# Gate and up of 17 feed-forward tiles as seven half-size block products, with two of the weight sums made by adding DMAs

## The chip, the cores and the metric

The kernel runs on one core of a Trainium2 chip. The metric is the device time of one execution in microseconds (us). Names of engines: PE is TensorE (matrix products; PEld is its loading of the stationary operand), DVE is VectorE, ACT is ScalarE, POOL is GpSimd, SP is SyncE, which here only issues transfers (DMAs).

## What is computed

One layer of a hybrid decoder for 512 tokens of width 1024, in float32. Two feed-forward blocks with 2816 hidden units stand around a mixing block of sixteen heads. The change is in the gate and up products of the two feed-forward blocks (`x @ wg` and `x @ wu`).

```python
def swiglu(x, wg, wu, wd):
    return (jax.nn.silu(x @ wg) * (x @ wu)) @ wd
...
        h = h + 0.5 * swiglu(rmsnorm(h, ffn1_norm[i]), ffn1_wg[i], ffn1_wu[i], ffn1_wd[i])
        a = rmsnorm(h, mix_norm[i])
        u = a @ w_in[i]
...
        h = h + mixed @ w_out[i]
        h = h + 0.5 * swiglu(rmsnorm(h, ffn2_norm[i]), ffn2_wg[i], ffn2_wu[i], ffn2_wd[i])
        gate = jax.nn.sigmoid(rmsnorm(h, ple_gate_norm[i]) @ ple_w_gate[i])
        e = rmsnorm(p[i] @ ple_w_proj[i], ple_norm[i])
        h = h + gate * e
```

## The kernel before

Every float32 product is made of three passes in the type float32r: an operand is split into a high part `hi` (a cast, on ScalarE) and a low part `lo` (operand minus `hi`, on VectorE), and `passes` gives high times high, high times low and low times high, which add up in one PSUM bank.

In `ffn` the 2816 hidden units are 22 tiles of 128, in chunks of 8, 7 and 7. For a tile and for each of gate and up, `weights` loads the [1024, 128] block of the weights in one 512 KB DMA on SP into a staging buffer (tag `st`, 3 slots), and `split` makes `hi` and `lo` (4 slots each). 24 matmuls (8 blocks of 128 inputs times 3 passes), each over all 512 tokens, fill one PSUM bank of the tag `gub` (4 banks). `hidden` then makes silu(gate) * up and splits it. After a chunk, the down projection runs over the chunk's tiles into the four banks of the tag `acc`, and the result is added to `h`. In the first block the first two tiles are computed while x arrives, and x is not yet normalized: the factor 1/rms of the tokens is multiplied onto the gate product (`R`, a row), and the other factor of it comes in after the down projection.

```python
        hi, lo = (self.nc.tile(self.sb, (P, 1024), F32R, tag, 4)[:, :a * n].rearrange("p (a c) -> p a c", a=a)
                  for tag in ("hi", "lo"))
```

The program isn't issued as it is written. `Plan.record` keeps every instruction with a cost and latencies from a table, and `Plan.issue` makes one list schedule of it: each engine takes, of the instructions whose operands and buffer slots are there in this model, the one that stands first in the program. The order of each engine's instructions is fixed by this; on the chip they run in that order, each when its operands are there. For this reason all instructions stand under one line of the profile, L296, and have to be told apart by the tiles that they write and read: `gub<-x,hi` is a gate or up product, `acc<-hi,k` or `acc<-hi,pt` one of the down projection, `lo<-st,hi` a split on VectorE, `hi<-st` a split on ScalarE. The profile leaves out buffer numbers, and a digit at the end of a tag with them (`x` is `x8`, `w` is `w2`, `k` is `k4`).

GpSimd does small arithmetic on statistics (`s`) and issues a handful of small DMAs at the start.

## Time and profile before

| what | value |
| --- | --- |
| time, three runs | 1122.46, 1122.73 and 1217.59 us; median 1122.73 us |
| span of the profiled execution | 1122.3 us |
| outside the span, against the median | 0.4 us |
| TensorE busy | 1106.8 us, 99%, 5635 matmuls |
| VectorE busy | 587.6 us, 52% |
| ScalarE busy | 493.9 us, 44% |
| GpSimd busy | 161.7 us, 14% |

The profiled execution is listed by its span alone, which is 0.2 and 0.4 us below the two lower runs; sums are made against the span, and the 0.4 us to the median are added. A busy engine isn't one at its peak: the records of matmuls overlap (a matmul of 512 columns has a record of 0.39 us), and what counts is the distance from one to the next. The granted clock is the share of TensorE's full speed of 2.4 GHz that it was given.

### The profile page before, as it was taken

The numbers are of one execution on the slowest core, as the hardware profiler recorded it, in microseconds if no ns is written. First come the engines' busy times: TensorE is split into PE (matmuls) and PEld (weight loads), VectorE is DVE, ScalarE is ACT, GpSimd is POOL, SyncE is SP. The second block draws the span as 40 slices with busy tenths as digits, with TensorE's granted clock in tenths as the row PEclk, the third lists the DMA queues.
The fourth block names the chain that finished last, engine by engine and source line by source line (L and its number), as shares of the span: only waits on it lengthen the run. The fifth ranks groups of instructions, "written<-read, shape, count | busy, mean of one in ns | idle before, by whom it ended". The sixth has DMA issues, their size and how long they took to land.

```text
span 1122.3 us, 15134 instructions
## 1 busy us (share of the span) xinstructions
PE 1106.8 (99%) x5635; PEld 941.9 (84%) x5635; DVE 587.6 (52%) x1121; ACT 493.9 (44%) x1017; POOL 161.7 (14%) x312
## 2 busy tenths in 40 slices
PE   9999999999999999999999999999999999999998
PEld 6888888888888988898999888888888888888887
DVE  5443343334443687889889887733333323333353
ACT  5332132222321767978988964522222221222252
POOL 2000000000000167553344511200000000000010
PEclk9999999999999999999999999999999999999999
DMA  7432333333343631312102232433223323332221
GB/s 215 123 97 94 94 94 95 100 88 112 95 107 84 213 119 39 76 30 58 36 25 72 100 125 73 137 103 102 94 75 113 94 85 103 104 103 85 90 80 66
DMA packets 143657, 106.60 MB, mean 95 GB/s; under 512 B 12624, under 2 KB 125296, under 8 KB 143584
## 3 DMA queue, kind: packets, MB, share of 16 engines
q1 hardware_dynamic: 143392, 105.55, 31.3%
q8 instruction: 45, 0.74, 0.3%
q14 instruction: 28, 0.23, 0.1%
q0 software_dynamic: 192, 0.08, 0.1%
HBM read 101.29 MB, written 4.33 MB: 94 GB/s over the span
## 4 chain that ended last, share of the span: by engine, by line
PE 87%; DVE 4%; POOL 2%; ACT 2%; issue 2%; DMA 1%; SPq 0%; POOLq 0%; ACTq 0%
PE gub L296 49%; PE acc L296 39%; DVE k L296 1%; POOL s L296 1%; ACT w L296 1%; DVE w L296 1%; POOL r L296 1%; POOL w L296 1%; ACT k L296 1%; DVE s L296 1%; DVE lo L296 0%; DMA st<-in_w_in 0%; DVE x L296 0%; DMA spill<-k 0%; DMA ident<-in_ident 0%
## 5 line engine op out<-in xcount | busy, mean ns | idle before, releaser
L296 PE MATMUL gub<-x,hi 128*128 128x512 f32 x1376 | 424.7, 390 | 0.0
L296 ACT CAST hi<-st 128x1024 fp32r<-128x1024 f32 (+4 forms) x171 | 166.1, 981 | 502.4 <-PE acc L296 181.6
L296 PEld LDWEIGHTS gub<-x,hi 128*128 128x128 f32 x1376 | 258.3, 188 | 53.1
L296 DVE TENSOR_TENSOR lo<-st,hi 128x1024 fp32r<-128x1024 f32 (+4 forms) x171 | 192.6, 1134 | 194.4 <-ACT hi L296 189.7
L296 PE MATMUL gub<-x,lo 128*128 128x512 f32 x688 | 267.8, 389 | 0.0
L296 PE MATMUL acc<-hi,x 128*128 128x256 f32 (+3 forms) x720 | 181.9, 329 | 0.0
L296 PE MATMUL acc<-hi,k 128*128 128x512 f32 (+1 forms) x512 | 166.0, 391 | 2.2 <-DVE k L296 2.0
L296 PEld LDWEIGHTS gub<-x,lo 128*128 128x128 f32 x688 | 129.2, 188 | 26.9
L296 POOL TENSOR_SCALAR s<-s 128x1 f32<-128x1 f32 (+3 forms) x65 | 18.6, 286 | 801.6 <-ACT k L296 755.9
L296 PEld LDWEIGHTS acc<-hi,x 128*128 128x128 f32 x720 | 123.3, 190 | 5.2
L296 PE MATMUL acc<-hi,pt 128*128 128x512 f32 x384 | 122.4, 395 | 0.0
L296 PE MATMUL acc<-lo,x 128*128 128x256 f32 (+3 forms) x360 | 117.5, 328 | 0.0
L296 PEld LDWEIGHTS acc<-hi,k 128*128 128x128 f32 x512 | 96.7, 190 | 19.8 <-issue 2.2
L296 PE MATMUL acc<-lo,k 128*128 128x512 f32 (+1 forms) x272 | 103.2, 383 | 0.0
L296 DVE TENSOR_TENSOR w<-w,gub 128x512 f32<-128x512 f32 x42 | 28.9, 688 | 135.6 <-PE gub L296 135.6
L296 PEld LDWEIGHTS acc<-hi,pt 128*128 128x128 f32 x384 | 72.3, 188 | 16.9
L296 PE MATMUL acc<-lo,pt 128*128 128x512 f32 x192 | 75.7, 394 | 0.0
L296 PEld LDWEIGHTS acc<-lo,x 128*128 128x128 f32 x360 | 68.2, 190 | 2.7
L296 ACT ACTIVATE w<-w,s 128x128 f32<-128x128 f32 (+1 forms) x96 | 53.8, 563 | 9.7 <-DVE s L296 9.3
L296 PEld LDWEIGHTS acc<-lo,k 128*128 128x128 f32 (+1 forms) x272 | 50.0, 184 | 8.5
L296 PE MATMUL gub<-ident,w 128*128 128x128 f32 (+2 forms) x316 | 52.4, 274 | 0.6 <-ACT w L296 0.2
L296 POOL TENSOR_TENSOR s<-s,mhalf 128x1 f32<-128x1 f32 (+3 forms) x61 | 49.4, 810 | 4.1
(154 smaller groups left out, 1198.9 us busy)
## 6 DMA issues: line engine op xcount, KB each, us to landing
st<-in_ffn_wg SPq DMA_DIRECT2D x42, 512.0 KB, 3.8
st<-in_ffn_wu SPq DMA_DIRECT2D x42, 512.0 KB, 3.9
st<-in_ffn_wd SPq DMA_DIRECT2D x40, 512.0 KB, 3.6
st<-in_w_in SPq DMA_DIRECT2D x48, 128.0 KB, 2.5
st<-in_w_in SPq DMA_DIRECT2D x8, 512.0 KB, 3.8
st<-in_w_out SPq DMA_DIRECT2D x8, 512.0 KB, 3.8
st<-in_ple_w_gate SPq DMA_DIRECT2D x8, 512.0 KB, 3.9
k<-in_x SPq DMA_DIRECT2D x16, 128.0 KB, 4.1
```

The costliest lines, as they stand in the source:

```text
L296: getattr(getattr(self.nc, op.eng), m)(*a, **k)
```

## The change

The 22 tiles become 11 pairs of 256 hidden units, p = 0 to 10, in chunks of pairs 0 to 3, 4 to 7 and 8 to 10. Pairs 0 to 2 of the first block and 0 and 1 of the second are computed as before (`gate_up`: 4 products of 24 matmuls over 512 tokens; the text calls them classic pairs). The other 17 pairs (8 and 9 of them) go through `gate_up7`.

There, the weights of a pair (gate and up side by side) and the transposed input are each cut into 2 by 2 blocks: the 1024 inputs into two halves, the 256 hidden units into two halves of 128, the 512 tokens into two halves of 256. Seven products of sums of blocks take the place of eight products of blocks. A product is 24 matmuls (gate and up, 4 blocks of 128 inputs, 3 passes) over 256 tokens, into one bank; a pair has 168 of them. The results are put together from the seven products by additions and subtractions on VectorE. The seven operands of the input (`x_operands`) are made once for each block, from a copy of the input that is put together by copying DMAs on SP (high part) and adding DMAs on GpSimd (low part).

For a pair, five 512 KB blocks of the weights are loaded on SP (`s`, `s3`, `a11`, `a22`, `a12`; the first two load the same block, quarter (1, 0)). Two DMAs issued by GpSimd read a block from DRAM and add it to what lies in the buffer (`accum_op`): quarter (0, 0) to `s3`, quarter (1, 1) to `s`. VectorE adds `a11` and later `a12` to `s`. Seven operands are split (`w7`, `w5`, `w6`, `w1`, `w4`, `w2`, `w3`, in the order in which their products run), each with one cast and one subtraction of 128x1024.

The tag `st` has 7 slots and holds the low parts too (before: 3 and 4); `k4` has 17 in place of 14. The down projection does the same products, two hidden tiles at a time, with a factor of 0.5; the row 1/rms is now multiplied onto gate and up both, in classic pairs, and onto the input's blocks for the others. To free buffers, the normalized embedding `e` is written to DRAM after its product and read back in the last stage, where its factor and gain are now multiplied on. The weights of gate and up come in a new layout from DRAM (`_quarters`), so that each block is one DMA of 4 KB rows. In the planner's table a matmul's cost changes, a GpSimd DMA costs 900 and the result of an adding DMA is due 4500 later. `L296` becomes `L304`.

```diff
-ST = 3
+ST = 7
 REST = 4
 STOP = "stop"
 PACE = 5250.0
 POOL_LO = ()
-K4 = 14
+K4 = 17
+CLASSIC = 2
...
-            return f * max(m / 1.2, self.cols(outs[0]) / 2.4) + 2.5
+            return f * max(m / 1.2 + 2.5, self.cols(outs[0]) / 2.4 + 13.5)
...
+        if method == "dma_start":
+            return 900.0
...
+        if "accum_op" in k:
+            op.lat = dict.fromkeys(op.lat, 4500.0)
...
+        hi, lo = (x[:, :a * n].rearrange("p (a c) -> p a c", a=a) for x in (self.hi(), self.st(F32R)))
...
+    def hidden_parts(self, a):
+        nc = self.nc
+        hi, lo = self.k4((P, 2, 512), F32R), self.k4((P, 2, 512), F32R)
+        nc.scalar.copy(hi, a)
+        nc.vector.tensor_sub(lo, a, hi.bitcast(F32))
+        return hi, lo
...
+    def gate_up(self, p, xT, quarters):
+        nc = self.nc
+        out = []
+        for r in range(2):
+            pair = []
+            for g in range(2):
+                w = self.st()
+                for c in range(2):
+                    nc.sync.dma_start(w[:, 512 * c:512 * c + 512], quarters[p, r, c, :, 512 * g:512 * g + 512])
+                w = self.split(w.rearrange("p (k c) -> p k c", k=NK), NK, P)
+                ps = self.gub()
+                for k in range(NK):
+                    for i, (a, b) in enumerate(self.passes(w, [y[:, k % 2] for y in xT[k // 2]])):
+                        nc.tensor.matmul(ps, lhsT=a[:, k, :], rhs=b, start=(k == 0 and i == 0),
+                                         stop=(k == NK - 1 and i == 2))
+                pair.append(ps)
+            out.append(pair)
...
+    def x_operands(self, xT, row=None):
+        nc = self.nc
+        V, G = nc.vector, nc.gpsimd
+        B = {}
+        for r, c in ((0, 1), (1, 1), (0, 0), (1, 0)):
+            b = B[r, c] = self.pt().bitcast(F32)[:, :1024].rearrange("p (k c) -> p k c", k=4)
+            cols = slice(256 * c, 256 * c + 256)
+            for n in range(2):
+                nc.sync.dma_start(b[:, 2 * n:2 * n + 2], xT[2 * r + n][0].bitcast(F32)[:, :, cols])
+            for n in range(2):
+                G.dma_start(b[:, 2 * n:2 * n + 2], xT[2 * r + n][1].bitcast(F32)[:, :, cols], accum_op=ALU.add)
+            if row is not None:
+                V.tensor_mul(b, b, row[:, None, cols].to_broadcast([P, 4, 256]))
...
+        def operand(i, src):
+            if i == 3:
+                hi, lo = (self.pt()[:, :1024].rearrange("p (k c) -> p k c", k=4) for _ in range(2))
+            else:
+                y = self.x8((P, 2, 4, 256))
+                hi, lo = y[:, 0], y[:, 1]
+            nc.scalar.copy(hi, src)
+            V.tensor_sub(lo, src, hi.bitcast(F32))
+            out[i] = hi, lo
...
+    def gate_up7(self, p, X, quarters):
+        nc = self.nc
+        V, G = nc.vector, nc.gpsimd
+        q = lambda r, c: quarters[p, r, c]
+        def load(r, c):
+            t = self.st()
+            nc.sync.dma_start(t, q(r, c))
+            return t
+        def operand(src):
+            hi, lo = self.hi(), self.st(F32R)
+            nc.scalar.copy(hi, src)
+            V.tensor_sub(lo, src, hi.bitcast(F32))
+            return hi, lo
+        def product(i, w, bank, first):
+            w = [x.rearrange("p (g k c) -> p g k c", g=2, k=4) for x in w]
+            for g in range(2):
+                for k in range(4):
+                    for n, (a, b) in enumerate(self.passes([x[:, g, k] for x in w], [x[:, k] for x in X[i]])):
+                        nc.tensor.matmul(bank[:, 256 * g:256 * g + 256], lhsT=a, rhs=b,
+                                         start=(first and g == k == n == 0), stop=(k == 3 and n == 2),
+                                         skip_group_check=True)
+        s, s3 = load(1, 0), load(1, 0)
+        G.dma_start(s3, q(0, 0), accum_op=ALU.add)
+        G.dma_start(s, q(1, 1), accum_op=ALU.add)
+        a11 = load(0, 0)
+        w7 = operand(s3)
+        w5 = operand(s)
+        rc, rb, rd, r1 = self.gub(), self.gub(), self.accb(), self.accb()
+        product(7, w7, rc, True)
+        V.tensor_add(s, s, a11)
+        a22 = load(1, 1)
+        w6 = operand(s)
+        product(5, w5, rb, True)
+        p5, c22 = self.w2(), self.w2()
+        nc.scalar.copy(p5, rb)
+        V.tensor_sub(c22, rc, p5)
+        w1 = operand(a11)
+        product(6, w6, rd, True)
+        a12 = load(0, 1)
+        w4 = operand(a22)
+        V.tensor_add(s, s, a12)
+        product(1, w1, r1, True)
+        z = self.w2()
+        nc.scalar.copy(z, r1)
+        V.tensor_sub(z, rd, z)
+        V.tensor_add(c22, c22, z)
+        acts = self.k4((P, 2, 512))
+        def hidden(c, j, half):
+            sg = self.w2()[:, :256] if c.space == PSUM else c[:, 0:256]
+            nc.scalar.activation(sg, c[:, 0:256], AF.Silu)
+            V.tensor_mul(acts[:, j, 256 * half:256 * half + 256], sg, c[:, 256:512])
+        w2 = operand(a12)
+        product(4, w4, rc, False)
+        hidden(c22[:], 1, 1)
+        c21 = self.w2()
+        V.tensor_add(c21, rc, z)
+        hidden(c21[:], 1, 0)
+        w3 = operand(s)
+        product(2, w2, r1, False)
+        hidden(r1[:], 0, 0)
+        product(3, w3, rb, False)
+        V.tensor_sub(z, rb, z)
+        hidden(z[:], 0, 1)
+        return acts
...
+        n = FF // (2 * P)
+        classic = CLASSIC + (started is not None)
...
+            if p < classic:
+                products = started if p == 0 and started else self.gate_up(p, xT, quarters)
+                raw.append(self.hidden(products, row))
+                if p == 0:
+                    X = self.x_operands(xT, row)
+            else:
+                parts()
+                raw.append(self.gate_up7(p, X, quarters))
+            if p in (3, 7, n - 1):
+                parts()
+                self.down(h, acts, p + 1 - len(acts), p == n - 1, wd, on_token)
...
-            e = self.x8((P, NT, 512), F32)
-            es.append(e)
...
+                e = self.w2()
+                nc.vector.tensor_copy(e, ps)
+                nc.sync.dma_start(spill[half][:, t], e)
...
+    e = [L.x8((P, NT, 512), F32) for _ in range(2)]
+    ge = gain("ple_norm")
     for half in range(2):
+        nc.sync.dma_start(e[half], spilled[half])
+        for t in range(NT):
+            nc.vector.scalar_tensor_tensor(e[half][:, t], e[half][:, t], e_r[t], ge[:, half * 512:half * 512 + 512],
+                                           op0=ALU.mult, op1=ALU.mult)
...
+    w = np.stack([wg[0], wu[0]]).reshape(2, 2, 4, P, FF // (2 * P), 2, P)
+    return np.ascontiguousarray(w.transpose(4, 5, 1, 3, 0, 2, 6)).reshape(FF // (2 * P), 2, 2, P, 1024)
```

Counted in the two programs: matmuls over 512 columns 3681 before and 2049 after, over 256 columns 584 and 3440; VectorE's additions and subtractions of 128x1024 142 and 279; ScalarE's casts of 128x1024 142 and 233; DMAs issued by GpSimd that add: 34 for weights (512 KB) and 16 for the input (256 KB), none before.

On VectorE, in the first block's second chunk, the order before: `lo` is a weight's low part, `w2` and `pt` hold the hidden units on their way, `k4_126` is the row 1/rms.

```order
L296 TENSOR_TENSOR lo_255<-st_253,hi_254 128x1024
L296 TENSOR_TENSOR w2_246<-gub_241,k4_126 128x512
L296 TENSOR_TENSOR lo_262<-st_260,hi_261 128x1024
L296 TENSOR_TENSOR w2_247<-w2_246,gub_245 128x512
L296 TENSOR_TENSOR lo_266<-st_264,hi_265 128x1024
L296 TENSOR_TENSOR pt_248<-w2_247,pt_248 128x512
```

A weight's split stands between any two steps of the hidden units.

After, at the turn from pair 5 to pair 6 of the same chunk. `k4_316` holds pair 5's hidden units, `w2_315<-gub_302,w2_315` is `z`, which reads pair 5's last product (product 3, bank `gub_302`), `st_329<-st_326,hi_328` is the low part of pair 6's first operand `w7`, `st_331` that of `w5`.

```order
L304 TENSOR_TENSOR k4_316<-w2_319 128x256
L304 TENSOR_TENSOR k4_316<-w2_322,acc_304 128x256
L304 TENSOR_TENSOR w2_315<-gub_302,w2_315 128x512
L304 TENSOR_TENSOR st_329<-st_326,hi_328 128x1024
L304 TENSOR_TENSOR st_331<-st_325,hi_330 128x1024
L304 TENSOR_TENSOR k4_316<-w2_315 128x256
L304 TENSOR_TENSOR st_325<-st_325,st_327 128x1024
```

So `z` of one pair stands ahead of the low part of the next pair's first operand. The same holds at five more turns (6 to 7 and 9 to 10 of the first block, and 5 to 6, 6 to 7 and 9 to 10 of the second). At the turns 4 to 5 and 8 to 9 of the first block and 2 to 3, 4 to 5 and 8 to 9 of the second, the low part of `w7` stands ahead of `z`, as here in the first block at 4 to 5:

```order
L304 TENSOR_TENSOR k4_285<-w2_291,acc_273 128x256
L304 TENSOR_TENSOR st_298<-st_295,hi_297 128x1024
L304 TENSOR_TENSOR w2_284<-gub_271,w2_284 128x512
L304 TENSOR_TENSOR st_300<-st_294,hi_299 128x1024
L304 TENSOR_TENSOR k4_285<-w2_284 128x256
```

Here `st_298` is that low part and `w2_284<-gub_271,w2_284` is `z`: the two have changed places against the turn from 5 to 6.

On TensorE the first block's second chunk begins before with the last products of a down projection (`acc_225`) and the first gate product (`gub_241`):

```order
L296 MATMUL acc_225<-hi_236,k4_205 128x512
L296 MATMUL acc_225<-lo_237,k4_205 128x512
L296 MATMUL acc_225<-hi_236,k4_205 128x512
L296 MATMUL gub_241<-x8_77,hi_239 128x512
L296 MATMUL gub_241<-x8_79,hi_239 128x512
L296 MATMUL gub_241<-x8_77,lo_240 128x512
L296 MATMUL gub_241<-x8_77,hi_239 128x512
L296 MATMUL gub_241<-x8_79,hi_239 128x512
```

A gate product follows without anything between, and its third matmul is the first to read a low part.

After, at the turn from pair 5 to 6: the last matmuls of product 3 (`gub_302`), then pair 6's product 7 (`gub_332`) and two matmuls of its product 5 (`gub_333`).

```order
L304 MATMUL gub_302<-pt_150,hi_320 128x256
L304 MATMUL gub_302<-pt_151,hi_320 128x256
L304 MATMUL gub_302<-pt_150,st_321 128x256
L304 MATMUL gub_332<-x8_144,hi_328 128x256 x2
L304 MATMUL gub_333<-x8_145,hi_330 128x256 x2
L304 MATMUL gub_332<-x8_144,st_329 128x256
L304 MATMUL gub_332<-x8_144,hi_328 128x256 x2
L304 MATMUL gub_332<-x8_144,st_329 128x256
```

The first two matmuls of product 7 and the two of product 5 need only the cast; the third of product 7 reads the low part `st_329`, and everything else stands behind it.

On SP the loads of a chunk stand in a row before, two for each tile:

```order
L296 DMA st_260<-in_ffn1_wg 128x8x128
L296 DMA st_264<-in_ffn1_wu 128x8x128
L296 DMA st_271<-in_ffn1_wg 128x8x128
L296 DMA st_275<-in_ffn1_wu 128x8x128
L296 DMA st_282<-in_ffn1_wg 128x8x128
```

Gate and up take turns, each in a slot of the 3 that a split has left.

After, for pair 6: `st_325` is `s`, `st_326` is `s3`, `st_327` `a11`, `st_336` `a22` and `st_343` `a12`.

```order
L304 DMA st_325<-in_quarters1 128x1024
L304 DMA st_326<-in_quarters1 128x1024
L304 DMA st_327<-in_quarters1 128x1024
L304 DMA st_336<-in_quarters1 128x1024
L304 DMA st_343<-in_quarters1 128x1024
L304 DMA st_356<-in_quarters1 128x1024
```

Five loads of whole blocks stand where four of gate and up columns stood, and each waits on SP for a free slot of the 7, with the ones behind it: `s` for the end of pair 5's product 6, `s3` for VectorE's split of pair 5's `w2`, `a11` for pair 5's product 1, `a22` for pair 5's product 2, `a12` for pair 6's product 7. On GpSimd the two adding DMAs of a pair follow one another, that of `s` first. They wait for the two loads to have landed, and the splits of `w7` and `w5` wait for them.

## Rows read from the trace of the kernel before

**Rows 1.** The page: span, busy line, granted clock, chain by engine.

```profile
span 1122.3 us, 15134 instructions
PE 1106.8 (99%) x5635; PEld 941.9 (84%) x5635; DVE 587.6 (52%) x1121; ACT 493.9 (44%) x1017; POOL 161.7 (14%) x312
...
PEclk9999999999999999999999999999999999999999
...
PE 87%; DVE 4%; POOL 2%; ACT 2%; issue 2%; DMA 1%; SPq 0%; POOLq 0%; ACTq 0%
```

**Rows 2.** The chain of waits, 100 to 340 us: start, us, what.

```profile
144.13 76.17 PE gub L296 x336
220.30 38.65 PE acc L296 x168
```

**Rows 3.** Stretch; busy us of PE, PEld, DVE, ACT, POOL; clock, DMA share.

```profile
144.13:220.30 76.17, 76.17 (x338) 63.09 (x337) 31.30 (x35) 21.88 (x28) 0.00 (x0) 1.00 0.33 100
```

**Rows 4.** The timeline of TensorE near the end: start, us, operation.

```profile
1112.15 0.40 PE L296 MATMUL acc<-hi,x 128*128 128x256 f32 x2
...
1117.19 0.40 PE L296 MATMUL acc<-hi,x 128*128 128x256 f32 x2
```

**Rows 5.** Weight loads by shape, 1112 to 1117.5 us: busy us, mean ns.

```profile
L296 PEld LDWEIGHTS acc<-hi,x 128*128 128x128 f32 x31 | 4.9, 192 | 0.0
```

**Rows 6.** Groups by shape, 100 to 300 us, VectorE: busy us, mean ns.

```profile
L296 DVE TENSOR_TENSOR lo<-st,hi 128x1024 fp32r<-128x1024 f32 x36 | 44.0, 1224 | 41.1 <-ACT hi L296 39.7
...
L296 DVE TENSOR_TENSOR w<-w,gub 128x512 f32<-128x512 f32 x11 | 7.6, 688 | 37.3 <-PE gub L296 37.3
```

**Rows 7.** The timeline of three engines, 144 to 151 us (parts).

```profile
143.90 1.23 DVE L296 TENSOR_TENSOR lo<-st,hi 128x1024 fp32r<-128x1024 f32 x1 [1.70 <-ACT hi L296]
145.04 0.74 DVE L296 SCALAR_TENSOR_TENSOR k<-acc,s,k 128x512 f32<-128x512 f32 x1
145.70 1.21 DVE L296 TENSOR_TENSOR lo<-st,hi 128x1024 fp32r<-128x1024 f32 x1
...
149.18 0.39 PE L296 MATMUL gub<-x,lo 128*128 128x512 f32 x1
...
149.38 1.06 ACT L296 CAST hi<-st 128x1024 fp32r<-128x1024 f32 x1 [4.16 <-PE gub L296]
...
149.61 0.69 DVE L296 TENSOR_TENSOR w<-gub,k 128x512 f32<-128x512 f32 x1 [2.70 <-PE gub L296]
150.47 1.23 DVE L296 TENSOR_TENSOR lo<-st,hi 128x1024 fp32r<-128x1024 f32 x1 [0.17 <-ACT hi L296]
```

**Rows 8.** DMA issues of the span: KB each, us to landing.

```profile
st<-in_ffn_wg SPq DMA_DIRECT2D x42, 512.0 KB, 3.8
...
st<-in_w_in SPq DMA_DIRECT2D x48, 128.0 KB, 2.5
...
x<-in_cmp_k_w SPq DMA_DIRECT2D x2, 1024.0 KB, 7.4
...
ident<-in_ident POOLq DMA_DIRECT2D x1, 64.0 KB, 3.4
```

**Rows 9.** DMA issues of 144 to 170 us alone.

```profile
st<-in_ffn_wg SPq DMA_DIRECT2D x3, 512.0 KB, 4.8
```

**Rows 10.** Waits of SP's queue: total us, times, longest.

```profile
SPq L296 <- DVE lo L296: 841.3, 168, 28.8
```

**Rows 11.** The timeline of TensorE around 402 us.

```profile
402.46 0.35 PE L296 MATMUL acc<-hi,k 128*128 128x256 f32 x1 [2.05 <-DVE k L296]
...
405.04 0.41 PE L296 MATMUL acc<-hi,k 128*128 128x256 f32 x1
405.26 0.41 PE L296 MATMUL acc<-lo,k 128*64 128x256 f32 x1
...
406.31 0.40 PE L296 MATMUL acc<-hi,x 128*128 128x256 f32 x2
```

**Rows 12.** Busy time of that stretch, with the granted clock.

```profile
400.00:405.00 5.00, 2.95 (x17) 2.78 (x16) 5.00 (x11) 2.88 (x6) 4.61 (x5) 0.79 0.45 155
```

More of the change, by code (lines that the diff above doesn't have):

```diff
@@ new lines, in hidden @@
+        out = self.k4((P, 2, 512))
+        for j, (pg, pu) in enumerate(products):
+            sg = self.w2()
+            if row is not None:
+                nc.vector.tensor_mul(sg, pg, row)
+                u = self.w2()
+                nc.vector.tensor_mul(u, pu, row)
+                pg, pu = sg, u
+            nc.scalar.activation(sg, pg, AF.Silu)
+            nc.vector.tensor_mul(out[:, j], sg, pu)
+        return out
+    def hidden_parts(self, a):
[4 more added lines that the diff above has]
+        return hi, lo
@@ new lines, in down, with mm @@
+    def down(self, h, acts, p0, final, wd, on_token):
+        nc = self.nc
+        n = len(acts)
+        for half in range(2):
+            cols = slice(half * 512, half * 512 + 512)
+            accs = [self.accb() for _ in range(NT)]
+            def mm(t, i, w):
+                for j in range(2):
+                    for k, (x, y) in enumerate(self.passes([a[:, j] for a in acts[i]], w)):
+                        nc.tensor.matmul(accs[t], lhsT=x[:, t * P:(t + 1) * P], rhs=y[:, j, :],
+                                         start=(i == 0 and j == 0 and k == 0),
+                                         stop=(i == n - 1 and j == 1 and k == 2))
+            tail = []
+            for i in range(n):
+                r0 = 2 * (p0 + i) * P
+                w = self.weights(wd[r0:r0 + 2 * P, cols].rearrange("(a p) c -> p a c", p=P))
+                if i < n - 2:
+                    for t in range(NT):
+                        mm(t, i, w)
+                else:
+                    tail.append((i, w))
+            for t in range(NT):
+                for i, w in tail:
+                    mm(t, i, w)
+                nc.vector.scalar_tensor_tensor(h[t][:, cols], accs[t], 0.5, h[t][:, cols], op0=ALU.mult, op1=ALU.add)
+                if half == 1 and final:
+                    on_token(t)
```

173 lines of the change are left out of this document (77 added, 96 removed).

## The prediction

> **What bounds the kernel now.** The page comes first: TensorE is busy for 1106.8 of 1122.3 us at the full granted clock, and the chain that ends last is 87% TensorE [rows 1]. The reader should see that only 15.5 us of the span are free of matmuls, so that a gain must come out of the matmuls' own time, and that any new wait of TensorE is paid in full. The chain of waits then shows the feed-forward block as TensorE's work alone: 336 gate and up matmuls in 76.17 us, then the down projection [rows 2]. That is 76.17 / 336 = 0.2267 us for a matmul over 512 columns, its distance to the next. In this stretch VectorE is busy for 31.30 of 76.17 us, ScalarE for 21.88, and the DMA share is 0.33 [rows 3]: there is room, and loads wait for slots (841.3 us of waiting by SP for VectorE's `lo` [rows 10]), which means that weights arrive ahead of their need. This is the cover that the change uses up.
>
> **What the matmuls give back.** The timeline near the end has matmuls over 256 columns: 14 steps of three between 1112.15 and 1117.19 us [rows 4], 5.04 / 42 = 0.120 us each. A weight load there has a record of 192 ns [rows 5], yet 31 of them lie in 5.5 us beside 16 others, so loads overlap one another and don't set the pace. A classic pair has 96 x 0.2267 = 21.77 us, a seven-product pair 168 x 0.120 = 20.16 us: 1.61 us less, and 17 x 1.61 = **27.4 us** less in all, if TensorE never waits.
>
> **Where TensorE will wait.** Inside a pair, operands are made one or more products (2.88 us) ahead. The turn between pairs is the place, since `s` and `s3` of the next pair get slots late and then need a load, an adding DMA, a cast and a subtraction one after the other. Of the 17 pairs, 6 follow a classic pair or a down projection; their loads can start 16 us or more ahead, and I cost them at nothing (the down projection, 38.65 us before [rows 2], hides the chain; without this cover each would cost what the other turns do). 11 turns are left.
>
> Durations for them: a subtraction of 128x1024 takes 1224 ns [rows 6], and the next VectorE instruction starts 1.14 us after it, after one of 512 columns 0.66 us; a cast takes 1.06 us, and the `lo` that reads it starts 0.03 us after it; VectorE starts 0.2 us after the time at which TensorE would issue its next matmul (149.18 + 0.23 = 149.41, then 149.61) [rows 7]. A 512 KB load lands after 3.8 us [rows 8], or 4.8 us with others close by [rows 9].
>
> No row of before shows an adding DMA. Call L the time from the landing of the plain load to the landing of the sum. The nearest rows: GpSimd's only DMA of some size, 64 KB, took 3.4 us, where SP's 128 KB took 2.5, so GpSimd's way costs at least 0.9 us more. With a 512 KB load's 3.8 us that makes **4.7 us** as the lower bound. An adding DMA reads its destination as well, as if 1024 KB moved: 7.4 + 0.9 = **8.3 us** as the upper one [rows 8]. With the 4.8 us of loads close together [rows 9] it is 5.7. I take 5.5, nearer to that, since the two additions and three loads of a turn come within some microseconds of each other. On the GpSimd way the Trainium skill, "DMA: Bandwidth & Descriptors", section "Anatomy of one DMA — SWDGE (gpsimd) path", has a fit of about 2.0 us plus the bytes over 436 GB/s, which would make 3.2 us (an estimate) of L; the row of 64 KB with its 3.4 us lies above that already. By that figure the sum below would be that of the lower bound. Against the change speaks "Collectives: The Full Stack" of the Trainium skill, section "The bandwidth ceiling: the fold count and why AG ≠ RS ≠ AR": an add in a DMA pays for two source reads; no row here shows one.
>
> *Five early turns* (second seven-product pair of a chunk). Count from the third matmul of the running pair's product 7; the third matmul of the next product 7 is due 20.16 us later. `s3` gets its slot when VectorE has split the running pair's `w2`: product 7 ends at 2.6, `a12` is loaded until 6.5, VectorE does `c22` after product 5 until 6.9, `s += a12` until 8.0 and the split until 9.3. The load of `s3` lands at 13.1, the sum at 13.1 + L, the cast ends at 14.3 + L and the low part at 15.5 + L. The stall is L - 4.65, so 0.8 us for L = 5.5, none at 4.7, 3.6 at 8.3. Five times 0.8 is 4 us.
>
> *Six late turns* (third and fourth pairs). Here the order of VectorE puts `z` of the running pair, which needs the end of product 3, ahead of the low part of the next `w7`. After product 3 TensorE has four matmuls (0.48 us) that need only casts, then it waits for 0.2 + 0.66 + 1.22 us less 0.48, about **1.7 us** with 0.06 us of handing over, even if the sums are long there. The loads can make it longer: VectorE comes late itself, after the low part of `w7` it has 10.26 us of work until the split of `w2` is done (seven instructions of 128x1024 at 1.14, one at 1.22 and three smaller ones), then 3.8 of load, L, 1.06 and 1.22 and some 0.35 of handing over follow: 16.7 + L against 20.16, a stall of L - 3.4, 2.1 us for L = 5.5, 4.9 at 8.3. Six times 2.1 is 12.6 us.
>
> *The clock.* After 2.05 us of idle TensorE in the mixing block the matmuls came 0.22 us apart in place of 0.12, until 406.31 us [rows 11], with a granted clock of 0.79 over 5 us that hold the idle time too [rows 12]: matmuls at the lower level of 1.2 GHz, here 3.85 us from 402.46 for 19 matmuls that would have taken 19 x 0.12 = 2.28 at the full level: some 1.6 us are lost. The late stalls are of just that length; I count 1.6 us for half of the six, **4.8 us**, with bounds of 0 and 11 x 1.6 = 17.6.
>
> **The rest**, all beside matmuls: GpSimd's 50 more DMAs are issued on an engine that does nothing in this stretch [rows 3], and behind them on its queue stand only the statistics of the next stage. SP's queue is in order, so a load that waits for its slot holds those behind it; the chain above has that in it. VectorE's load in a pair comes to ten of 128x1024 and nine smaller ones, 17 of 20 us, where it was 9 of 22, so VectorE nearly binds, and this is why the late chain starts 10.26 us late. The input's operands are made beside two classic pairs (43 us). The embedding's return (two loads of 1 MB, 7.4 us at worst [rows 8], and eight VectorE instructions) lies in the last stage beside its 192 matmuls (43.5 us at 0.2267). I take nothing for all this, with bounds of 5 us on either side, since the buffers that it moves also change orders in the mixing block.
>
> **The sum**: 1122.3 - 27.4 + 4 + 12.6 + 4.8 = 1116.3 us of span. The profiled span lies 0.4 us below the median, so the time is 1116.7, say **1117 us**.
>
> **Rivals.** A difference under about 2% (1100.3 to 1145.2 us) is what a measurement here can't well tell from none.
>
> *A, the forecast*: most of the gain is lost at the turns, within 2%. With L = 4.7 and no lower clock it is 1122.7 - 27.4 + 6 x 1.7 = 1105.5; if the loads of a turn each take 4.8 us, 11 us more, 1128; with the clock at all eleven turns 13 more than the forecast, 1130. With the 5 us of the rest it spans 1101 to 1135. Chance 0.66.
>
> *B, slower*: the adding DMA is slow, and every turn also loses the clock. At L = 8.3 the turns cost 5 x 3.6 + 6 x 4.9 = 47.4 and the clock 17.6: 1122.7 - 27.4 + 65 = 1160. It is decided by L: 2% is passed where 11 L - 43.7 + 17.6 - 27.4 = 22.5, at L of about 6.9 us. For it: adding reads twice the bytes, and the 1 MB load took 7.4 us. Against: that load started among others, and new blocks come in longer rows. Chance 0.18.
>
> *C, faster by over 2%*: the turns cost less than 5 us in all, so about 1098. It needs the sums to land early, L under 4.7, and the six stalls behind `z` to shrink to under 0.8 us, or else a gain in the rest. The order on VectorE speaks against it. The skill's fit for L, above, gives half of the condition only, and alone 1105.5. Chance 0.14.
>
> *D, the seven products save nothing*: each matmul over 256 columns waits for its weight load of 192 ns. Then a pair takes 168 x 0.192 = 32.3 us and the kernel 1122.7 + 17 x 10.5 = 1301 us. The 0.120 us pace near the end speaks against it, with as many weight loads as matmuls. Chance 0.02.
>
> The range takes A, the lower half of B and the upper part of C: 1097 to 1152 us. Chances: faster 0.14, within 2% 0.66, slower 0.20.
>
> **What the changed kernel's profile would show.** Matmuls over 256 columns 0.12 us apart inside a pair, and the pairs at 20.2 us from third matmul to third matmul where nothing stalls. At late turns an idle time of TensorE of some 2 us before the third matmul of product 7, released by VectorE's `st`, with `z` just ahead of it; at early turns under 1 us. DMA issues of GpSimd into `st` of 512 KB with the landing time that L needs. Granted clock below 9 in slices of the two blocks. TensorE's busy time would be down by some 25 us, idle time up from 15 to 30 us or more. I am wrong if the landing time is far from 5.5 us, if idle time lies inside the pairs and not between them, or if entries of chunks stall.

## Result and the profile after

The changed kernel takes 1193.17 us (median of 3 runs, 1189.14 to 1196.38) against 1122.73: a ratio of 1.0624, 95% interval 1.0583 to 1.0665. It is slower by 70 us, above the predicted range, and slower where a small gain was forecast. The profiled execution is the fastest of the three; its span of 1187.2 us is what the sums below are made against.

The page after, lines as in [rows 1]:

```profile
span 1187.2 us, 18145 instructions
PE 1112.3 (94%) x6859; PEld 998.4 (84%) x6859; DVE 763.4 (64%) x1323; ACT 585.0 (49%) x1132; POOL 205.1 (17%) x358
...
PEclk9899998999889999999999999998999899988999
...
PE 31%; DMA 7%; DVE 3%; ACT 2%; issue 1%; POOL 1%; SPq 0%; ACTq 0%; POOLq 0%; DVEq 0%
```

TensorE is busy for 5.5 us longer than before, though it has 27 us less to do at full clock, and it is free for 74.9 us where it was for 15.5. The clock line has lost its even row of nines: the 8s lie in slices of the two feed-forward blocks. The chain has DMA in it with 7%.

What TensorE waited for (total, times, longest), and the DMA issues that answer to [rows 8]:

```profile
PE gub L304 <- ACT hi L304: 47.2, 21, 4.8
```

```profile
st<-in_quarters SPq DMA_DIRECT2D x85, 512.0 KB, 4.1
...
st<-in_quarters POOLq DMA_DIRECT2D x34, 512.0 KB, 7.3
```

A plain load takes 4.1 us (3.8 before), an adding DMA 7.3. The wait named, for ScalarE's cast of a weight operand, holds the turns. The first of them, on TensorE's timeline:

```profile
169.15 0.29 PE L304 MATMUL gub<-pt,st 128*128 128x256 f32 x1
174.01 1.74 PE L304 MATMUL gub<-x,hi 128*128 128x256 f32 x4 [4.58 <-ACT hi L304]
```

The stall stands before the first matmul of product 7, at the cast, not before the third. It occurs at exactly the 11 turns that the prediction counted: 4.58, 4.33, 4.54, 4.06 and 4.04 us at the five early ones, 4.83, 2.79, 3.17, 2.98, 2.65 and 4.14 at the six late ones, 42.1 us in all. Around this turn, by stretches (busy times of PE, PEld, DVE, ACT, POOL; clock, DMA share, GB/s), as [rows 12]:

```profile
160.00:164.00 4.00, 4.00 (x36) 4.00 (x35) 2.21 (x5) 1.00 (x2) 0.85 (x1) 1.00 0.88 307
164.00:170.00 6.00, 5.43 (x46) 5.22 (x44) 1.25 (x3) 0.80 (x2) 0.86 (x1) 1.00 0.99 188
172.00:175.00 3.00, 0.84 (x3) 0.55 (x3) 1.01 (x1) 1.99 (x2) 0.00 (x0) 0.60 0.02 8
175.00:180.00 5.00, 5.00 (x25) 5.00 (x26) 5.00 (x7) 2.95 (x4) 0.00 (x0) 0.55 0.00 0
```

The first two rows differ in what the DMA engines do: up to 164 us plain loads move 307 GB/s, then, while the two adds run, only 188 GB/s with the engines full (0.99). From 157 to 176 us the two kinds took the same share of the engines, the adds (`q0`) for half the bytes of the plain loads (`q1`; packets, MB, share):

```profile
q0 software_dynamic: 288, 1.05, 31.0%
q1 hardware_dynamic: 576, 2.10, 30.6%
```

So a byte that is added costs the DMA engines twice the time of a byte that is loaded here. The last row of the stretches shows the price that follows a stall: a clock of 0.55, nearly the level of 1.2 GHz, and 25 matmuls in 5 us, 0.20 us each in place of 0.12. Summed over the 11 turns, the matmuls after a stall take about 29.6 us longer than at 0.12 us each (1.9 to 3.3 us a turn).

The chain of waits through two turns of the second block (start, us, what):

```profile
900.49 7.84 DMA st<-in_quarters
...
909.36 1.05 ACT hi L304
...
910.45 7.00 PE gub L304 x46
...
918.68 0.69 DVE w L304
919.36 2.28 DVE st L304 x2
...
921.66 4.92 DMA st<-in_quarters
...
926.64 0.47 issue
...
927.13 6.36 DMA st<-in_quarters
...
934.51 1.05 ACT hi L304
...
935.60 7.94 PE gub L304 x46
```

This is one period of a loop: products 7 and 5 (7.00 us), `c22` (0.69), `s += a12` and the split of `w2` (2.28), the load of the next `s3` (4.92), its add (6.36, after 0.47 of issue), the cast (1.05), products 7 and 5. The rest of the period is another split, the cast of the other operand and handing over. TensorE is in this chain for 7.00 of the 25.15 us from 910.45 to 935.60; for the rest it works on what is left or waits.

### The profile page after: what moved, and what is told of

The parts are those of the page before. It is cut to its first block, busy times and chain, and to the rows that moved or that the text cites. A ratio compares the mean times of both kernels' runs of the same rounds, so it can differ in the third digit from the quotient of the medians.

```text
span 1187.2 us, 18145 instructions
## 1 busy us (share of the span) xinstructions
PE 1112.3 (94%) x6859; PEld 998.4 (84%) x6859; DVE 763.4 (64%) x1323; ACT 585.0 (49%) x1132; POOL 205.1 (17%) x358
## 5 line engine op out<-in xcount | busy, mean ns | idle before, releaser
L304 DVE TENSOR_TENSOR st<-st,hi 128x1024 fp32r<-128x1024 f32 (+4 forms) x218 | 254.3, 1176 | 209.6 <-ACT hi L304 197.8
L304 ACT CAST hi<-st 128x1024 fp32r<-128x1024 f32 (+4 forms) x218 | 215.9, 1008 | 319.3 <-DMA st<-in_quarters 153.4
L304 PE MATMUL acc<-hi,k 128*128 128x512 f32 (+1 forms) x832 | 261.9, 389 | 1.1 <-DVE k L304 1.0
L304 PE MATMUL gub<-x,hi 128*128 128x256 f32 x816 | 173.5, 313 | 44.4 <-ACT hi L304 44.1
L304 PE MATMUL acc<-hi,x 128*128 128x256 f32 (+3 forms) x784 | 204.1, 335 | 0.0
L304 PEld LDWEIGHTS gub<-x,hi 128*128 128x128 f32 x816 | 145.1, 217 | 50.4 <-ACT hi L304 49.7
L304 PEld LDWEIGHTS acc<-hi,k 128*128 128x128 f32 x832 | 155.7, 188 | 31.8 <-issue 1.2
L304 PE MATMUL acc<-st,k 128*128 128x512 f32 (+1 forms) x432 | 164.2, 383 | 0.0
L304 PE MATMUL acc<-x,hi 128*128 128x256 f32 x816 | 147.3, 282 | 0.0
L304 PEld LDWEIGHTS acc<-hi,x 128*128 128x128 f32 x784 | 135.1, 189 | 8.0
L304 PE MATMUL acc<-st,x 128*128 128x256 f32 (+3 forms) x392 | 131.1, 335 | 0.1
L304 POOL DMA_DIRECT2D st<-in_quarters x34 | 29.4, 865 | 571.8 <-DMA st<-in_quarters 370.8
L304 PEld LDWEIGHTS acc<-x,hi 128*128 128x128 f32 x816 | 125.6, 189 | 0.0
L304 PE MATMUL gub<-x,st 128*128 128x256 f32 x408 | 122.7, 305 | 0.1
L304 PE MATMUL acc<-x,st 128*128 128x256 f32 x408 | 114.9, 283 | 0.4 <-DVE st L304 0.4
L304 PE MATMUL gub<-k,hi 128*128 128x512 f32 x288 | 92.0, 401 | 3.1 <-ACT hi L304 3.1
L304 PEld LDWEIGHTS acc<-st,k 128*128 128x128 f32 (+1 forms) x432 | 79.4, 184 | 14.9 <-DVE st L304 0.2
L304 PEld LDWEIGHTS gub<-x,st 128*128 128x128 f32 x408 | 86.5, 214 | 0.3 <-DVE st L304 0.3
L304 PEld LDWEIGHTS acc<-st,x 128*128 128x128 f32 x392 | 74.1, 189 | 5.0 <-DVE st L304 0.5
L304 PEld LDWEIGHTS acc<-x,st 128*128 128x128 f32 x408 | 76.8, 189 | 0.6 <-DVE st L304 0.6
L304 PEld LDWEIGHTS gub<-k,hi 128*128 128x128 f32 x288 | 55.3, 194 | 14.9 <-ACT hi L304 3.5
L304 ACT ACTIVATE w<-w 128x256 f32<-128x256 f32 (+4 forms) x84 | 36.8, 440 | 52.1 <-DVE w L304 51.9
```

What stands on the lines that cost most here:

```text
L304: getattr(getattr(self.nc, op.eng), m)(*a, **k)
```

## The experiments

Ratios are to the kernel before on the same chip, with 95% intervals.

**Is it the time of the adds?** Three kernels shrink or replace the adding DMAs of the weights.

```diff
-        G.dma_start(s3, q(0, 0), accum_op=ALU.add)
-        G.dma_start(s, q(1, 1), accum_op=ALU.add)
+        G.dma_start(s3[:, :64], q(0, 0)[:, :64], accum_op=ALU.add)   # e1 and, for s alone, e2
+        G.dma_start(s[:, :64], q(1, 1)[:, :64], accum_op=ALU.add)
...
+        G.dma_start(s3, q(0, 0), held=True)   # e3: overwrites; the planner's order is held
+        G.dma_start(s, q(1, 1), held=True)
```

> Both adding DMAs of a pair add 64 of the 1024 columns only (32 KB in place of 512 KB); the rest of the two sums is left out. Order of all instructions as in the changed kernel. Theory S (the two adds, one behind the other, hold all 16 DMA engines at about half of a plain load's pace, 5.9 us for the two, and so the sum of s3 lands late): the landing falls from 7.3 to under 4 us, the five early turns stall by nothing, the six late ones by 1.7 us for z; idle time at the turns falls from 42 to about 10 us, the time lost at 1.2 GHz from 30 to about 10: 1132 to 1150 us. Rival P (GpSimd's way is slow whatever it moves): the landing stays near 7 us and the time above 1180. Rival V (slots and VectorE set the turns): idle time at the turns stays above 30 us, time above 1170.

> Only the adding DMA of s, which stands first on GpSimd, adds 64 columns in place of 1024 (the rest of that sum is left out); that of s3 is whole. Theory S: s3's add no longer waits for the engines behind s's add, so it takes 1.7 us to start and about 3 to move: 5 us in place of 7.9; early turns stall by under 0.5 us, late ones by 1.7 to 2: 1135 to 1155 us. If the landing of s3's sum is set by its own way or size alone, it stays at 7 us or more and the time above 1175.

> The two DMAs on GpSimd overwrite s3 and s in place of adding to them (the sums are left out); same queue, size and order. Theory S: a plain 512 KB takes half the engine time of an add, so 1.7 + 2 x 1.6 = 4.9 us from the issue of the first to the landing of the second; landing 4 to 5.5 us, time 1135 to 1158 us. Rival P (GpSimd's way, not the adding, is slow): landing stays at 7 us, time above 1175.

Measured: e1 1128.87 us, 1.0052 [1.0037, 1.0067]; e2 1157.45, 1.0313 [1.0296, 1.0330]; e3 1150.92, 1.0248 [1.0226, 1.0270]. Their DMA issues by GpSimd, in this order:

```profile
st<-in_quarters POOLq DMA_DIRECT2D x34, 32.0 KB, 3.0
```

```profile
st<-in_quarters POOLq DMA_DIRECT2D x17, 512.0 KB, 5.5
...
st<-in_quarters POOLq DMA_DIRECT2D x17, 32.0 KB, 3.4
```

```profile
st<-in_quarters POOLq DMA_DIRECT2D x34, 512.0 KB, 4.7
```

With two small adds no stall of a turn is above 1.1 us. One full add takes 5.5 us and leaves 19.8 us of stalls; with two in a row the median is 7.3 and 42.1 us are left. Plain transfers of the same size in the same place take 4.7, and four turns still stall by more than 1 us, 12.8 us together. The order of all engines is the same in these runs. Of the 64 us between e1 and the changed kernel, 22 come with moving the bytes at this place (e3), and the other 42 with adding them in place of overwriting.

**What is left without the turns?** All pairs are made classic, with the input's parts back in their old buffers (e4), then with the planner's old matmul cost (e10), or with the embedding kept in buffers (e11); and the changed kernel gets the old cost (e14).

```diff
-CLASSIC = 2
+CLASSIC = 11
...
-            return f * max(m / 1.2 + 2.5, self.cols(outs[0]) / 2.4 + 13.5)
+            return f * max(m / 1.2, self.cols(outs[0]) / 2.4) + 2.5   # e10, e14
```

> All 11 pairs of both blocks are classic, so no seven products, no sums and no operands of x; x's parts lie in x8 and m in k4 as before the change. What stays of the change: pairs and chunks of 8, 8 and 6 tiles, the new layout and 7 slots, the planner's new numbers, 17 slots of k4, e by way of DRAM. If the 11 us that the mixing block grew by and the 4 us at the start come from these, 1130 to 1140 us; if they come from the seven products and their operands, 1120 to 1126 us.

> All pairs classic as before (1130.6 us), with the planner's old cost of a matmul. If the 7 us that stay there come from the new numbers (another order in the mixing block), 1122 to 1126 us; if not, 1129 to 1132.

> All pairs classic, with e kept in its buffers as before the change in place of the way by DRAM. If the 7 us come from e's stores, loads and the later multiplications, 1122 to 1126 us; if not, 1129 to 1132.

> The changed kernel with only the planner's cost of a matmul put back. If the 7 us that it makes in the all-classic kernel add to what the turns cost, 1183 to 1188 us in place of 1193; if the turns are ordered worse by it, 1190 or more.

Measured: e4 1130.59, 1.0063 [1.0048, 1.0078]; e10 1123.08, 1.0005 [0.9995, 1.0014]; e11 1130.18, 1.0063 [1.0048, 1.0078]; e14 1194.65, 1.0649 [1.0633, 1.0664]. The 7 us of the classic version come from the planner's cost of a matmul alone, which changes the order of other stages; the embedding's way over DRAM costs nothing. In the changed kernel the old cost gains nothing: the terms don't add.

With e4 as the base, the distances between the starts of down projections in the traces say where the changed kernel and e1 lose. Each cell is the stage's time less e4's, plus 1.61 us for each seven-product pair in it:

| stage (seven-product pairs) | changed kernel | e1 |
| --- | --- | --- |
| first block to its first down projection (1) | 8.6 | 7.5 |
| to the second (4) | 19.5 | 3.4 |
| to the third (3) | 13.4 | 1.8 |
| mixing block, second block's first chunk (2) | 14.3 | 7.6 |
| to the second (4) | 16.8 | 3.8 |
| to the third (3) | 14.3 | 1.5 |
| end | 0.8 | 1.0 |
| sum | 87.7 | 26.6 |

87.7 less 27.4 is the 60.3 us between the spans of 1187.2 and 1126.9. Rows 2, 3, 5 and 6 are the turns: stalls and slow matmuls there come to 19.3, 13.4, 16.8 and 14.3 us in the changed kernel. Row 4 has one turn, of 4.54 and 3.1 us, which leaves 6.6.

So rows 1 and 4 show a second loss, of 7 to 9 us a block, that is there with small adds as well. It lies where a block begins, and the trace of the changed kernel shows two causes. In the first block TensorE waits for the factors 1/rms, which GpSimd works out; ScalarE has their four sums ready by 26.8 us, but on GpSimd the third and fourth stand behind adding DMAs for the input's operands, and those wait for their loads:

```profile
32.89 1.24 POOL L304 DMA_DIRECT2D pt<-k  x1 [1.27 <-DMA pt<-k]
34.21 0.18 POOL L304 TENSOR_SCALAR s<-s 128x1 f32<-128x1 f32 x1
```

```profile
36.98 0.47 PE L304 MATMUL acc<-ident,w 128*128 128x128 f32 x1 [4.09 <-DVE w L304]
```

In e4, without these DMAs, GpSimd has done the same statistics by 21.8 us, and TensorE doesn't wait there. At the second block's begin TensorE waits 3.07 us (until 769.47) for the cast of a classic pair's weight, and ScalarE for its load; these loads of 256 KB (745 to 771 us) stand beside the copies and adds of the input, with the DMA engines at nine tenths or more for most of it, and land after 8.1 us, in e4 after 3.4:

```profile
768.37 1.04 ACT L304 CAST hi<-st 128x1024 fp32r<-128x1024 f32 x1 [9.46 <-DMA st<-in_quarters]
```

```profile
st<-in_quarters SPq DMA_DIRECT2D x11, 256.0 KB, 8.1
```

**Is the clock a cost of its own?** Matmuls without a use are put in at the turns, with the planner's order changed by them (e5, 36 a turn) or kept (e9, meant as 22 a turn).

```diff
+        for _ in range(fill):
+            nc.tensor.matmul(rc[:, 0:256], lhsT=X[1][0][:, 0, 0:P], rhs=X[1][0][:, 1], start=True, stop=True, ...)
         product(7, w7, rc, True)
```

> The changed kernel with 36 matmuls over 256 columns of x's own parts ahead of product 7 of each of the eleven pairs that follow a seven-product pair (4.3 us of work into a bank that product 7 then starts anew), so that TensorE works on through most of the wait. Theory C (the 30 us lost after the stalls are a lower clock granted because TensorE stood idle): granted clock full after the turns, time lost there under 6 us, idle at the turns 42 down to under 8 us, and the time falls by about 20 us in spite of 47 us of added work: 1165 to 1178 us. Rival (the slow matmuls after a turn have another cause, such as the busy DMA engines or weight loads): they stay slow and the time is 1193 or more.

> Fillers again, 22 matmuls (2.6 us) at each of the eleven turns, now costed at nothing by the planner, so that the order of every engine stays that of the changed kernel but for them; 2.6 us is less than every stall there, so they delay nothing. Theory C (idle TensorE is what lowers the clock, and the slow products 7 and 5 behind a stall are part of the chain that makes the next one): less time at 1.2 GHz, 46 matmuls of products 7 and 5 back to 5.5 us from 7 to 8, and 10 to 25 us less: 1168 to 1183 us. If the turns are a loop of loads, additions and splits alone, as the chain of the other filler run has it, 1190 or more.

Measured: e5 1204.45, 1.0720 [1.0697, 1.0743]; e9 1190.59, 1.0600 [1.058, 1.0621]. e9 isn't the test that it was meant to be: to the planner its fillers cost nothing, and it put 44 of them at the first turn of four chunks, 22 at three turns and none at the other four. The order of all other instructions is that of the changed kernel. The mean clock rises from 0.968 to 0.979, but the time hardly falls. TensorE's wait for the casts, and the two turns of the first block's third chunk:

```profile
PE gub L307 <- ACT hi L307: 37.7, 14, 7.3
```

```profile
313.02 5.43 PE L307 MATMUL gub<-x 128*128 128x256 f32 x44
...
345.67 0.79 PE L307 MATMUL gub<-x,hi 128*128 128x256 f32 x2 [7.08 <-ACT hi L307]
```

At the four turns with 44 fillers TensorE isn't idle, and products 7 and 5 behind them run at 0.12 us a matmul. Yet the next product 7 begins 28.6, 27.4, 28.1 and 27.6 us after theirs, where it was 27.7, 26.0, 25.2 and 27.4 in the changed kernel: the lower clock is gone there, and the next turn comes no sooner. Since 44 fillers take 5.3 us and the stalls there were 4.0 to 4.6, they hold TensorE up a little themselves. In e5 the chain has, from one turn to the next, no TensorE in it:

```profile
935.02 8.35 DMA st<-in_quarters
...
943.44 1.05 ACT hi L304
...
951.27 1.23 DVE st L304
952.51 3.21 DMA st<-in_quarters
```

The adding DMA, the cast, VectorE's work until slots are free, and the next load set the pace there. So the 29.6 us of low clock don't come back by filling the gaps while that loop binds; a clean run, 22 fillers at each turn and no other change, was not made. e5 can't be read further, since some 50 instructions of VectorE changed places.

**Does the order of the two adds matter?** `s3` is needed first and its add stands second.

```diff
-        s, s3 = load(1, 0), load(1, 0)
+        s3, s = load(1, 0), load(1, 0)
```

> Loads and adding DMAs of s3 stand ahead of those of s (s3 feeds product 7, which comes first), all else as in the changed kernel; the planner then orders anew. Theory S: s3's add no longer stands behind another one, 1.7 + 3 us, and s's add has 2.9 us more until product 5; idle at the turns falls from 42 to 10 to 20 us: 1135 to 1165 us. If only the sum of the engines' work in a turn counts, whatever the order, 1180 us or more.

Measured: 1170.97, 1.0423 [1.0403, 1.0442], above the range expected, though 22 us better. Nine of the eleven stalls are now 1.2 to 3.5 us and two are under 0.3, 20.9 us in all; the adds still take 7.4 us.

**Other hands for the sums.** GpSimd adds loaded blocks (e7), and the input's operands are also made one pair later (e8, `if p == classic - 2`).

```diff
+        s, a11, a22 = load(1, 0), load(0, 0), load(1, 1)
+        s3 = self.st()
+        G.tensor_tensor(s3, s, a11, ALU.add)
+        G.tensor_tensor(s, s, a22, ALU.add)
```

> No adding DMAs for weights: four plain loads for a pair, and GpSimd itself adds a11 and a22, which are loaded anyway, to quarter (1, 0). By its 1.30 us for 128x512 one sum is about 2.6 us. Theory S: the DMA engines' work in a turn falls from 13 to 6 us, stalls at the turns come to under 10 us in all and the clock stays up: 1118 to 1132 us, at or below the run with small adds. Rival G (additions on GpSimd hold up VectorE or are themselves too slow, over 4 us): 1150 us or more.

> As the run with GpSimd's additions, and the seven operands of x are made one pair later in the first block. If the 4 us lost at the start come from the copies of x on SP ahead of the first loads, they go: 3 to 5 us below that run. If they come from the first loads' own 5.9 us landing, no difference.

Measured: e7 1133.46, 1.0092 [1.0076, 1.0108]; e8 1132.17, 1.0080 [1.0063, 1.0096]. Without adding DMAs of the weights 60 us come back, but not the gain. VectorE's groups by shape, 140 to 380 us (busy us, mean ns), of the changed kernel and then of e7:

```profile
L304 DVE TENSOR_TENSOR st<-st,hi 128x1024 fp32r<-128x1024 f32 x62 | 75.1, 1223 | 68.2 <-ACT hi L304 63.1 <-issue 4.7
...
L304 DVE TENSOR_TENSOR k<-w 128x256 f32<-128x256 f32 x21 | 8.9, 423 | 4.9 <-ACT w L304 4.8
```

```profile
L304 DVE TENSOR_TENSOR st<-st,hi 128x1024 fp32r<-128x1024 f32 x62 | 82.6, 1334 | 36.3 <-ACT hi L304 27.6 <-PE acc L304 8.0
L304 DVE TENSOR_TENSOR k<-w 128x256 f32<-128x256 f32 x21 | 17.1, 814 | 4.0 <-ACT w L304 4.0
```

The same instructions last longer beside a GpSimd addition (2.42 us each): at one turn of e7, while GpSimd adds from 870.54 to 875.48,

```profile
871.21 2.01 DVE L304 TENSOR_TENSOR k<-w 128x256 f32<-128x256 f32 x1 [0.49 <-ACT w L304]
874.05 2.52 DVE L304 TENSOR_TENSOR st<-st,hi 128x1024 fp32r<-128x1024 f32 x1 [0.83 <-ACT hi L304]
```

in place of 0.42 and 1.22. The Trainium skill, "SBUF — State Buffer", section "SBUF: two separate sides", says that a VectorE operation with two SBUF inputs and a GpSimd operation that reads SBUF hold a port pair in turn, each for a whole instruction; these rows agree. The later operands of e8 gave 1.3 us and not the 3 to 5 expected.

**Sums that are made ahead.** The sums of late pairs are made in DRAM, far ahead, and loaded plainly. In e12 they are made as early as the queue lets them, in e13 after the first chunk's loads and with the old planner cost (kept in e15 to e17), in e15 spread one pair at a time with a tiny GpSimd instruction ahead that waits for a given pair, in e16 with three classic pairs a block, in e17 with fewer sums beside the end of the first block.

```diff
+        G.tensor_scalar(self.small(), gate[:, 0, 511:512], 1.0, None, op0=ALU.mult)   # e15 to e17
...
+                t = self.dram.tile([P, 1040], F32, name=f"spill_{quarters.tensor.name}_{p}_{i}")[:, :1024]
+                G.dma_start(t, quarters[p, 1, 0])
+                todo.append((t, quarters[p, b[0], b[1]]))
...
+        for t, b in todo:
+            G.dma_start(t, b, accum_op=ALU.add)
...
+            nc.sync.dma_start(s, self.sums[quarters.tensor.name, p, 0])
+            nc.sync.dma_start(s3, self.sums[quarters.tensor.name, p, 1])
...
+        classic = 3   # e16, e17
```

> The two sums of each of the eleven pairs that follow a seven-product pair are made in DRAM, by a copy and an adding DMA on GpSimd, one chunk or more ahead (the second block's during the first); the pair then loads s and s3 as plain blocks, and the planner puts the low part of w7 ahead of z. x's operands one pair later in the first block. Theory S (late sums and what hangs on them cost the change its gain): stalls at the turns go but for under 5 us, 1130.6 - 27.4 + 5 to 12 for starts and turns: 1106 to 1118 us. Rival M (the DMA engines as a whole are too busy with 18 MB of copies and additions more): loads land late, 1125 or more.

> Sums of the eleven pairs in DRAM as in the other run with sums ahead, but started only after the first chunk's loads (behind pair 3's own adding DMAs on GpSimd), and with the planner's old cost of a matmul. Theory S: the start is as in the changed kernel (no 24 us of idle TensorE before 62 us), turns stall by under 5 us in all, the mixing block is as before: 1122.7 - 27.4 + 5 for the starts + 5 to 12 for turns: 1104 to 1115 us, faster than both. Rival M (copies and additions, now within 90 to 330 us, delay the loads of the first block): 1120 or more.

> Sums in DRAM ahead, the planner's old cost, and now each pair's sums are held back on GpSimd until an earlier pair's hidden units are there (a one-element operation that reads them), so that the copies and additions spread over 105 to 370 us, the last three pairs' in the second block. Theory S: the stalls of 3.0 and 1.7 us at the first block's turns go, 5 to 8 us below the other run with sums held late: 1119 to 1126 us. Rival M (spreading doesn't help, any copy and addition beside the loads costs): 1127 or more.

> As the gated run, with three classic pairs in place of two in the second block and its operands of x made one pair later, behind the first loads. The 4 us of idle time at the second block's start (third weight loads behind the copies of x on SP) go, for 1.6 us more of matmuls: 2 to 5 us below the gated run, 1115 to 1123 us, which would be at or below the kernel before. If the start waits for something else, 1 to 3 us above the gated run.

> As the gated run with three classic pairs, with the sums of the second block's pair 3 left away (it is no longer behind a seven-product pair there) and those of its pair 6 moved from the first block's last chunk into the second block. The idle time of 6.5 us before the first block's last down projection, whose weights landed after 10.9 us beside six copies and additions, goes with the clock that it lost: 5 to 9 us below 1127.4 us, 1118 to 1122.5 us. If those weights are late for another reason (the mixing block's constants on SP ahead of them), 1125 or more.

| kernel | us | ratio [95%] |
| --- | --- | --- |
| e12 | 1155.10 | 1.0282 [1.0264, 1.0299] |
| e13 | 1129.46 | 1.0061 [1.0046, 1.0075] |
| e15 | 1129.62 | 1.0052 [1.0035, 1.0068] |
| e16 | 1127.43 | 1.0044 [1.0027, 1.0061] |
| e17 | 1121.09 | 0.9984 [0.9970, 0.9997] |

Only e17 came within the time that its theory expected. e12 moves the stalls to the start, where its copies run beside the first loads (TensorE's two largest waits):

```profile
PE acc L304 <- DVE w L304: 13.2, 4, 8.5
PE acc L304 <- DMA k<-in_x: 10.6, 6, 4.9
```

In e13 the first block still stalls at two turns (2.99 and 1.70 us), the second block at none. Its second chunk (four pairs), after e13, the changed kernel and e4, by stretches as above:

```profile
852.00:933.00 81.00, 81.00 (x675) 80.96 (x674) 64.17 (x74) 42.12 (x55) 0.00 (x0) 1.00 0.37 130
```

```profile
885.00:983.00 98.00, 87.26 (x676) 85.85 (x675) 64.49 (x74) 42.23 (x55) 5.16 (x6) 0.93 0.50 141
```

```profile
845.00:932.00 87.00, 87.00 (x386) 72.03 (x385) 29.55 (x28) 24.07 (x28) 0.00 (x0) 1.00 0.30 103
```

The windows are cut to whole microseconds; from first to last matmul the chunk takes 80.64 us in e13 (20.16 a pair), 97.4 in the changed kernel and 87.04 in e4. So the matmuls' gain is there to the full where the sums come early. What e15 and e16 lost again was a stall of 7.36 and 6.48 us (until 341 and 340 us), ahead of the last down projection of the first block, whose weights came late beside the copies; e17 moves those sums elsewhere. The loads of `wd` between 300 and 345 us, of e16 and of e17:

```profile
st<-in_ffn_wd SPq DMA_DIRECT2D x4, 512.0 KB, 10.9
```

```profile
st<-in_ffn_wd SPq DMA_DIRECT2D x6, 512.0 KB, 6.1
```

The stall is gone, and e17 is just below the kernel before, by less than 2 us. A stall of 4 us where the second block begins stays in e13 and in e15 to e17. The third classic pair of e16 and e17 was to remove it and didn't: on SP the copies of the input still stand ahead of the loads that TensorE waits for.

## Why the prediction was wrong, point by point

- **Matmuls, -27.4 us: right.** e13's chunk shows the 20.16 us of a pair. Rival D falls.
- **The 11 turns: places right, L wrong.** The step that failed is "I take 5.5". The add that a turn waits for is the second one, that of `s3`; it takes 6.4 to 8.9 us at the 11 turns, 7.6 on average, and with some 0.5 of issue L is about 8.1, near my upper bound. The turns cost 42.1 us where I had 16.6. With that L the formulas L - 4.65 and L - 3.4 make 5 x 3.45 + 6 x 4.7 = 45.5; the sum comes near, its parts don't: early turns took 4.3 us, late ones 3.4. I priced one transfer at a time from rows of lone transfers, added the bytes up to 8.3 as the far end, and then took a value near the 5.7 of the shorter way. At a turn two adds run one behind the other, and the engines are full at 188 GB/s. e2 shows 5.5 us for one full add behind a small one, which is what I took where two run. The fit of the Trainium skill, "DMA: Bandwidth & Descriptors", section "Anatomy of one DMA — SWDGE (gpsimd) path", makes 3.2 us for 512 KB (an estimate); the runs lie above it, with 4.7 for a plain transfer (e3) and 7.3 for an adding one. "Collectives: The Full Stack" of the Trainium skill, section "The bandwidth ceiling: the fold count and why AG ≠ RS ≠ AR", says that an add needs two source reads; the trace agrees, with 31.0% of the engines for 1.05 MB of adds and 30.6% for 2.10 MB of loads.
- **`z` ahead of the low part: there, but hidden and smaller.** I made it a floor of 1.7 us at late turns. The stalls of the changed kernel end at the cast of `w7`, which comes before it. With small adds (e1) the late turns wait for 0.73 to 1.05 us, at five of the six before the first matmul that reads the low part; with a shorter wait at a cast beside it, 1.2 to 1.4 us a turn.
- **The clock, 4.8 us: mis-sized, and not a free-standing term.** I took 1.6 us from a 2 us stall [rows 11]; after stalls of 2.7 to 4.8 us it was 1.9 to 3.3, 29.6 in all, above my bound of 17.6. Where fillers kept the clock up in e9, the next turn came no sooner, which fits a loop of load, add, cast and split that sets the pace. How the 72 us divide between loop and clock can't be told apart by these runs.
- **"The rest", 0 with bounds of 5: wrong.** I wrote of GpSimd's new DMAs that only the statistics of the next stage stand behind them; in the first block the statistics of that very block stand among them, and TensorE waits for these. And "beside two classic pairs" was no cover for the input's operands in the second block, since their copies and adds delay the loads of those pairs. The two blocks' first chunks lost 8.6 and 6.6 us, and the last stage 0.8. Of this the two waits are 4.09 and 3.07 us, and matmuls at the lower clock follow them (granted clock 0.50 from 37 to 42 us and 0.66 from 769.5 to 774.5). The traces show these causes; no run took them out by themselves, and the remainder is open. 4.6 us more of the span are in e4 (e10: the planner's matmul cost).
- **The sum**, of the spans: 1122.3 - 27.4 + 42.1 + 29.6 + 15.2 + 0.8 + 4.6 = 1187.2, as measured. It is a tally and no test, since the terms were read from the same trace, and e14 shows that the planner's 4.6 doesn't come off by itself. Against my 1116.3 the turns make 25.5 us of the miss, the clock 24.8, the rest 16.0 and the planner 4.6. Rival B, at 1160, was the right case by kind and place: slow adds, and the clock lost at every turn; its threshold of L = 6.9 was passed. Its price was short by the larger clock loss and the rest.

## What to carry over

A transfer put into a queue beside others is to be priced by the work that the DMA engines do in that window, not by the landing time of a lone one; an add counted double here. What is put on a queue that runs in order can hold up what stands behind it, however small. Where a buffer's release, its load and the next use form a loop, write the loop's period down first: it, and not a sum of stalls, sets the pace, and filling one gap moves the wait to the next. A saving of 1.6 us a pair is only had if everything ahead of it is made early, and a planner's cost that is changed along with it can move stages that the change doesn't touch.

## What was not expected of the hardware

- While adding DMAs run, all engines are full at 188 GB/s where plain loads move 307; a 512 KB add takes 5.5 us behind a small one and 7.3 as one of two (medians), a plain transfer on the same queue 4.7.
- Stalls of 2.7 to 4.8 us cost 1.9 to 3.3 us more in matmuls at the lower clock.
- GpSimd additions of two SBUF tiles hold VectorE's instructions up, from 1.22 to 2.52 us and from 0.42 to 2.01.
- The runs of e17 spread from 1117.8 to 1126.1 us, those of the kernel before on the same chip from 1122.1 to 1125.0.
